# Plain float32 matmuls on unsplit weights in place of three float32r products of split halves, in a one-layer hybrid decoder kernel

## The chip, the cores and the metric

The kernel runs on one core of a Trainium2 chip. The metric is device time in microseconds (us) of one execution. Three runs of the kernel before took 1446.25, 1450.61 and 1451.01 us; their median is 1450.61 us.

## The reference, cut to what matters

One layer on 256 tokens of width 2048, batch 1, all float32: a mixer (half gated delta net, half RWKV7), a cross attention to 256 memory rows, and a squared-ReLU feed-forward part of width 8192.

```python
u = rmsnorm(h, mix_norm_w)
p = u @ w_in                                  # 2048 x 7440
h = h + concat(deltanet(p[:4112]), rwkv7(p[4112:])) @ w_out
h = h + cross_attention(rmsnorm(h), rmsnorm(mem), wq, wk, wv, wo)
u = rmsnorm(h, ffn_norm_w)
h = h + square(relu(u @ w1)) @ w2             # 2048 x 8192, 8192 x 2048
out = rmsnorm(h, final_norm_w)
```

Nearly all arithmetic is in the products with w_in, w_out, wq, wk, wv, wo, w1 and w2. They are the projections that the change is about. The mixer's scans, triangular inverses, transposes and attention scores are small float32 matmuls of their own, which the change leaves as they are.

## The kernel before, in words

Weights stream from HBM in blocks of 512 KB, each once: two k tiles of 128 rows by 512 columns, or for w1 eight k tiles by 128 columns. `weights` (L228) issues the DMA of a block into a tile `raw` (pool `wp`, five buffers) on SP's queue. It then splits the block in two parts, in two steps of 128x512: ScalarE casts the high half, `A.copy(hi, w)` (L239, tile `whi`), and VectorE subtracts it from the original to make the low half (L240, tile `wlo`, shown at L110, the line of the helper `tt`). Both halves have the type float32r. The activations are split in the same way, by `lhs_split` (L187, tile `xhl`), `tok_T` (L1035, tile `hhl`), `dn_out` (`dhl`), `split_out` (`ohl`), the attention's output (`oahi`, `oalo`) and `relu2` (L1186, tiles `fhi`, `flo`).

A projection is then three float32r products summed in PSUM: high by high, high by low, low by high. There are two forms.

- `gemm` (L244) puts tokens on the partitions of the result: for each k tile and each half of the tokens (m) three products of 128x128 by 128x512 (L254 to L256). It serves w_in, w_out, wq, wk, wv, wo and w2. `gemm_rows` (L205) is the same for the last 512 columns of w2, with the first 128 tokens done before the others.
- `gemm_T` (L261) puts columns of w1 on the partitions: for each k tile one product 512 columns wide, W_hi by (x_hi, x_lo) side by side (L273), and one 256 columns wide, W_lo by x_hi (L272, L275). The two halves of the 512-wide result are added after the sum, in `relu2`.

The low-rank group at the start (the loop at L393, "lora") has products 272 columns wide (L402 to L404).

Three PSUM banks (`ps_g`) serve these products. The order of all instructions on each engine comes from the Tile framework's scheduler, which fits the projections between the steps of the scans and inverses; `tc.high_priority(3000)` brings the loads and splits of weights forward. The first half of the program is the mixer, with w_in's products as filler between its small matmuls (`ps_s`, `ps_x`); then come output projection and cross attention, and from about 727 us on there is only the feed-forward part: four times 32 `gemm_T` groups of w1 and four `gemm` groups of w2.

The steps of the triangular inverse that the text names are, on TensorE, L541, L553, L558, L563 and L567: each works on what ScalarE and VectorE made of the step before. They have the lines L504, L516, L521, L526 and L530 after the change.

Of the kernel before, what the change touches and what calls it, by code (L numbers as in the profile page):

```python
# [10 lines left out]
F32R = mybir.dt.float32r  # L11
# [16 lines left out]
WB = 3  # L28
# [12 lines left out]
def host_layout(inp):  # L41
# [63 lines left out]
def body(ctx, tc, I, out, dbg=None, upto=99):  # L105
# [24 lines left out]
    wp = ctx.enter_context(tc.tile_pool(name="wp", bufs=5))  # L130
    lx = ctx.enter_context(tc.tile_pool(name="lx", bufs=4))
# [39 lines left out]
    # derived per-channel scalars  # L171
# [15 lines left out]
    def lhs_split(raws, wname, pool, tag):  # L187
        """raw^T (times the norm's weight) split in two float32r parts, four k tiles a tile, as they are asked for."""
        res = {}

        def get(kt, m):
            j = kt // 4
            if j not in res:
                raw = raws(j)
                t = pool.tile([P, 4, 2, S], F32R, tag=tag, bufs=4, name=nm("xhl"))
                for q in range(4):
                    w = C(wname, 4 * j + q)
                    act(t[:, q, 0], raw[:, q], AF.Copy, scale=w)
                    stt(t[:, q, 1], raw[:, q], w, t[:, q, 0].bitcast(F32), ALU.mult, ALU.subtract)
                res[j] = t  # L200
            return tuple(res[j][:, kt % 4, i, m * P:(m + 1) * P] for i in range(2))

        return get

    def gemm_rows(lhs, wblk, evac, kbs, his, los):  # L205
        """the same, the first 128 tokens before the others, from weights that all stay."""
        kbs, w = list(kbs), []
        for m in range(2):
            acc = bank("g")
            for i, kb in enumerate(kbs):  # L210
                if m == 0:
                    with tc.high_priority(3000):
                        raw = wp.tile([P, KB, NB], F32, tag="raw", name=nm("raw"))
                        nc.sync.dma_start(out=raw, in_=wblk[kb])
                        hi, lo = his(), los()
                        A.copy(hi, raw)
                        tt(lo, raw, hi.bitcast(F32), ALU.subtract)
                    w.append((hi, lo))
                hi, lo = w[i]
                for q in range(KB):  # L220
                    first, last = i == 0 and q == 0, i == len(kbs) - 1 and q == KB - 1
                    xh, xo = lhs(kb * KB + q, m)
                    T.matmul(acc, lhsT=xh, rhs=hi[:, q], start=first, stop=False)
                    T.matmul(acc, lhsT=xh, rhs=lo[:, q], start=False, stop=False)
                    T.matmul(acc, lhsT=xo, rhs=hi[:, q], start=False, stop=last)  # L225
            evac(m, acc)

    def weights(src, a, b, parts):  # L228
        """a block of weights [128, a, b] in two float32r parts."""
        with tc.high_priority(3000):  # L230
            raw = wp.tile([P, a, b], F32, tag="raw", name=nm("raw"))
            nc.sync.dma_start(out=raw, in_=src)
            res = []
            n = a // parts
# [9 lines left out]
    def gemm(lhs, wblk, n, evac, kbs=None):  # L244
        """[256 tok, n] = lhs^T @ W: three float32r products stand for the float32 one."""
        acc = [bank("g") for _ in range(2)]
        kbs = list(kbs if kbs is not None else range(NKT // KB))
        for kb in kbs:
            w = weights(wblk[kb], KB, n, KB)
            for q in range(KB):  # L250
                for m in range(2):
                    first, last = kb == kbs[0] and q == 0, kb == kbs[-1] and q == KB - 1
# [4 lines left out]
                    if last:  # L257
                        evac(m, acc[m][:, :n])


    def gemm_T(rhs, wblk, evac):  # L261
        """(x W)^T in four parts of 128 columns, [128 col, (W x_hi, W_hi x_lo)]; rhs(kt) is (x_hi, x_lo)^T, 512 wide."""
        for j in range(4):
            acc = bank("g")
            for b in range(2):
                w = weights(wblk[j, b], 8, P, 2)
                for k in range(8):
                    first, last = b == 0 and k == 0, b == 1 and k == 7
                    x = rhs(8 * b + k)
                    xf = x.rearrange("p a t -> p (a t)")  # L270
# [5 lines left out]
            evac(j, acc)  # L276
# [22 lines left out]
    def rms(src, name):  # L299
        """1 / rms of the rows of src[:, m, :]."""  # L300
# [8 lines left out]
    def tpose4(o, ins):  # L309
        """up to four 128x128 transposes into one bank."""  # L310
# [40 lines left out]
    xl = lhs_split(lambda j: xraw[:, 4 * j:4 * j + 4], "mixw", lx, "lx")  # L351
# [9 lines left out]
    # the clock of the array rises and the functions' table loads while the first operands are on their way  # L361
# [29 lines left out]
    with tc.manual_schedule(engines={mybir.EngineType.Activation, mybir.EngineType.DVE}):  # L391
        for kb in range(NKT // KB):
            raw = wl[kb]  # L393
            whi = sp_.tile([P, KB, LORA], F32R, tag="whi", bufs=3, name=nm("whi"))
            wlo = sp_.tile([P, KB, LORA], F32R, tag="wlo", bufs=3, name=nm("wlo"))
            A.copy(whi, raw)
            tt(wlo, raw, whi.bitcast(F32), ALU.subtract)
            for m in range(2):
                for q in range(KB):
                    first, last = kb == 0 and q == 0, kb == NKT // KB - 1 and q == KB - 1  # L400
                    xh, xo = xl(kb * KB + q, m)
                    T.matmul(acc[m], lhsT=xh, rhs=whi[:, q], start=first, stop=False)  # L402
                    T.matmul(acc[m], lhsT=xh, rhs=wlo[:, q], start=False, stop=False)
                    T.matmul(acc[m], lhsT=xo, rhs=whi[:, q], start=False, stop=last)  # L404
# [30 lines left out]
    # gates of the deltanet: [tok, chunk, head]  # L435
# [35 lines left out]
    inv = [0]  # L471

    def inverse(B, pool, pool2):
        """B is overwritten with the inverse of I + (its strictly upper part); what lies below its diagonal is zero.

        X12 = -X11 B12 X22 for blocks of 2 to 128, the larger ones on tiles of the array."""
# [11 lines left out]
        def quarters(t, n):  # L488
            """the quarters 11, 12, 22 of the diagonal blocks of 2n: [q, block, row, column]."""
# [94 lines left out]
    def rw_shift(pt, c0, names, blks):  # L584
        """columns c0.. of the projection [tok, col] to shifted [col, tok] tiles of two blocks."""
# [12 lines left out]
    def rw_unit(u, r, k, v):  # L598
# [59 lines left out]
        # bonus * v  # L658
# [8 lines left out]
        # scores  # L667
# [21 lines left out]
        # [tok, .] forms  # L689
# [57 lines left out]
        # group norm, bonus, gate  # L747
# [94 lines left out]
    def dn_unit(g, kq, v2):  # L842
# [6 lines left out]
        # norms per token: [tok, (k/q), chunk, head]  # L849
# [21 lines left out]
        # decays, scores  # L871
# [72 lines left out]
        # norm over the head, times silu(z)  # L944
# [16 lines left out]
    def dn_out(g, ob):  # L961
# [4 lines left out]
        t = lx.tile([P, 4, 2, S], F32R, tag="lx", name=nm("dhl"))  # L966
        for q in range(2):
            bb = bank()
            tpose4(bb, [ob[:, 4 * c + 2 * q + i] for i in range(2) for c in range(2)])
            b2 = bb.rearrange("p (a b) -> p a b", a=2)  # L970
            hi, lo = (t[:, 2 * q:2 * q + 2, i] for i in range(2))
            act(hi, b2, AF.Copy, scale=dnwh)
# [252 lines left out]
```

## Time and profile before

| | before |
|---|---|
| runs | 1446.25, 1450.61, 1451.01 us |
| median | 1450.61 us |
| profiled execution: span from its first to its last instruction | 1442.5 us |
| TensorE busy | 1414.8 us, 98% |
| VectorE busy | 950.1 us, 66% |
| ScalarE busy | 780.8 us, 54% |
| DMA | 252.88 MB, mean 175 GB/s |

The page gives the span of the profiled execution, and no time of its own for it beside that. The median of the runs is 8.1 us above the span, which is what lies around the span (start and end of the program). TensorE's matmuls are pipelined: the duration of one record (some 390 ns for 512 columns) is longer than the distance between the starts of two. So what one matmul costs is read from starts, not from durations.

### The profile page before, as it was taken

The numbers are of one execution on the slowest core, as the hardware profiler recorded it, in microseconds if no ns is written. First come the engines' busy times: TensorE is split into PE (matmuls) and PEld (weight loads), VectorE is DVE, ScalarE is ACT, GpSimd is POOL, SyncE is SP. The second block draws the span as 40 slices with busy tenths as digits, with TensorE's granted clock in tenths as the row PEclk, the third lists the DMA queues.
The fourth block names the chain that finished last, engine by engine and source line by source line (L and its number), as shares of the span: only waits on it lengthen the run. The fifth ranks groups of instructions, "written<-read, shape, count | busy, mean of one in ns | idle before, by whom it ended". The sixth has DMA issues, their size and how long they took to land.

```text
span 1442.5 us, 22496 instructions
## 1 busy us (share of the span) xinstructions
PE 1414.8 (98%) x8284; PEld 1168.9 (81%) x8284; DVE 950.1 (66%) x1799; ACT 780.8 (54%) x1491; POOL 50.6 (4%) x66
## 2 busy tenths in 40 slices
PE   9999999999999989999999999999999999999997
PEld 7877788787876868887788888888888888888886
DVE  7748574869587685767676655666556665566664
ACT  7656454555456454566565544555445554455553
POOL 0010001100010000000000000000000000000000
PEclk9999999999999999999999999999999999999999
DMA  7444433454366464556465556555665555655554
GB/s 281 157 145 152 135 121 112 147 177 144 102 200 207 138 190 146 166 173 212 136 209 186 190 192 197 185 187 189 193 197 186 185 190 194 195 182 187 191 188 146
DMA packets 90688, 252.88 MB, mean 175 GB/s; under 512 B 20673, under 2 KB 29393, under 8 KB 90193
## 3 DMA queue, kind: packets, MB, share of 16 engines
q1 hardware_dynamic: 70304, 243.96, 51.2%
q10 hardware_dynamic: 19920, 6.42, 1.8%
q8 instruction: 65, 1.06, 0.3%
q0 software_dynamic: 352, 1.06, 0.2%
q14 instruction: 47, 0.38, 0.1%
HBM read 244.72 MB, written 6.69 MB: 174 GB/s over the span
## 4 chain that ended last, share of the span: by engine, by line
PE 82%; DMA 7%; DVE 6%; ACT 3%; issue 2%; SPq 0%; POOL 0%; ACTq 0%; POOLq 0%; DVEq 0%
PE ps_g L273 16%; PE ps_g L255 16%; PE ps_g L254 15%; PE ps_g L256 15%; PE ps_g L272 8%; DVE wlo L110 2%; PE ps_s L675 2%; DMA scr<-Sc 1%; DMA xc<-inv 1%; DMA mraw<-in_memT_dram 1%; PE ps_x L312 1%; DMA g<-scr 1%; DVE xtmp L110 1%; DMA junk<-in_mem_dram 1%; PE ps_s L312 1%
## 5 line engine op out<-in xcount | busy, mean ns | idle before, releaser
L110 DVE TENSOR_TENSOR wlo<-raw,whi 128x512 fp32r<-128x512 f32 x848 | 583.3, 691 | 388.1 <-ACT whi L239 386.8
L239 ACT CAST whi<-raw 128x512 fp32r<-128x512 f32 x848 | 523.4, 621 | 489.8 <-DVE wlo L110 203.7
L273 PE MATMUL ps_g<-hhl,whi 128*128 128x512 f32 x1024 | 357.6, 398 | 0.2 <-ACT whi L239 0.2
L272 PE MATMUL ps_g<-hhl,wlo 128*128 128x256 f32 x960 | 269.9, 281 | 0.0
L273 PEld LDWEIGHTS ps_g<-hhl,whi 128*128 128x128 f32 x1024 | 188.4, 188 | 42.5 <-ACT whi L239 0.5
L255 PE MATMUL ps_g<-wlo,xhl 128*128 128x512 f32 x512 | 209.9, 410 | 8.4 <-DVE wlo L110 8.3
L256 PE MATMUL ps_g<-whi,xhl 128*128 128x512 f32 x512 | 202.0, 395 | 0.0
L256 PE MATMUL ps_g<-whi,flo 128*128 128x512 f32 x480 | 186.7, 389 | 0.0
L255 PE MATMUL ps_g<-wlo,fhi 128*128 128x512 f32 x480 | 186.7, 389 | 0.0
L254 PE MATMUL ps_g<-whi,xhl 128*128 128x512 f32 x512 | 180.8, 406 | 3.4 <-ACT whi L239 3.4
L272 PEld LDWEIGHTS ps_g<-hhl,wlo 128*128 128x128 f32 x960 | 181.5, 189 | 2.8 <-ACT hhl L122 0.2
L254 PE MATMUL ps_g<-whi,fhi 128*128 128x512 f32 x480 | 151.3, 389 | 0.0
L255 PEld LDWEIGHTS ps_g<-wlo,xhl 128*128 128x128 f32 x512 | 96.6, 189 | 37.7 <-DVE wlo L110 18.2
L254 PEld LDWEIGHTS ps_g<-whi,xhl 128*128 128x128 f32 x512 | 94.6, 189 | 26.7 <-ACT whi L239 5.9
L256 PEld LDWEIGHTS ps_g<-whi,xhl 128*128 128x128 f32 x512 | 96.7, 189 | 18.8 <-issue 0.7
L255 PEld LDWEIGHTS ps_g<-wlo,fhi 128*128 128x128 f32 x480 | 90.1, 188 | 18.8
L256 PEld LDWEIGHTS ps_g<-whi,flo 128*128 128x128 f32 x480 | 90.1, 188 | 18.7
L254 PEld LDWEIGHTS ps_g<-whi,fhi 128*128 128x128 f32 x480 | 90.1, 188 | 18.6
L113 DVE SCALAR_TENSOR_TENSOR cy<-ps_x,colt,cy 128x255 f32<-128x255 f32 (+2 forms) x72 | 34.2, 476 | 10.9 <-ACT cy L122 10.3
L1191 ACT CAST fhi<-hid 128x256 fp32r<-128x256 f32 x64 | 26.1, 408 | 9.5 <-DVE hid L113 0.8
L113 DVE SCALAR_TENSOR_TENSOR hid<-hid 128x256 f32<-128x256 f32 x64 | 27.2, 425 | 2.2
L113 DVE SCALAR_TENSOR_TENSOR h<-ps_g,rf,h 128x512 f32<-128x512 f32 (+1 forms) x34 | 22.8, 712 | 8.0 <-PE ps_g L225 8.0
(360 smaller groups left out, 1540.7 us busy)
## 6 DMA issues: line engine op xcount, KB each, us to landing
raw<-in_w_dram SPq DMA_DIRECT2D x256, 512.0 KB, 3.5
raw<-in_w_in_dram SPq DMA_DIRECT2D x112, 512.0 KB, 3.5
raw<-in_w_out_dram SPq DMA_DIRECT2D x32, 512.0 KB, 3.5
raw<-in_wk_dram SPq DMA_DIRECT2D x8, 512.0 KB, 3.5
mraw<-in_memT_dram SPq DMA_DIRECT2D x8, 512.0 KB, 3.6
raw<-in_wq_dram SPq DMA_DIRECT2D x8, 512.0 KB, 3.4
raw<-in_wv_dram SPq DMA_DIRECT2D x8, 512.0 KB, 3.7
raw<-in_wo_dram SPq DMA_DIRECT2D x8, 512.0 KB, 3.5
```

The source lines that it names most:

```text
L110: return (e or V).tensor_tensor(o, a, b, op=op)
L113: return V.scalar_tensor_tensor(o, a, s, b, op0=op0, op1=op1)
L239: A.copy(hi, w)
L254: T.matmul(acc[m][:, :n], lhsT=xh, rhs=w[q][0], start=first, stop=False)
L255: T.matmul(acc[m][:, :n], lhsT=xh, rhs=w[q][1], start=False, stop=False)
L256: T.matmul(acc[m][:, :n], lhsT=xl, rhs=w[q][0], start=False, stop=last)
L272: T.matmul(acc[:, 0:S], lhsT=w[k][1], rhs=x[:, 0], start=False, stop=False)
L273: T.matmul(acc, lhsT=w[k][0], rhs=xf, start=first, stop=last)
L312: T.transpose(out=o[:, j * P:(j + 1) * P], in_=a, identity=ident)
L675: T.matmul(bb[hl][:, 256 * i:256 * i + 256], lhsT=BK[hs, j, i, cs], rhs=AR[hs, j, :, cs], start=True, stop=True)
L1191: A.copy(hi[:, j], t)
```

## The change

All splitting goes. `weights` is the DMA alone, and its tile `raw`, plain float32, is the operand. `gemm` and `gemm_rows` issue one plain float32 matmul per k tile and token half in place of three float32r ones; `gemm_T` issues one of 256 columns in place of a 512 and a 256 column one; the lora loop one in place of three. Activations are scaled by the norm's weight only, with the scaling shared between ScalarE and VectorE. `relu2` reads the 256 finished columns, one ReLU on ScalarE and one square on VectorE, in place of five instructions. `split_out` loads its tile by DMA without a split. The pools `wp` and `lx` have eight buffers each (5 and 4 before; the tiles of `lx` are half as large).

```diff
-    wp = ctx.enter_context(tc.tile_pool(name="wp", bufs=5))
-    lx = ctx.enter_context(tc.tile_pool(name="lx", bufs=4))
+    wp = ctx.enter_context(tc.tile_pool(name="wp", bufs=8))
+    lx = ctx.enter_context(tc.tile_pool(name="lx", bufs=8))
...
-    def weights(src, a, b, parts):
+    def weights(src, a, b, pool=None, tag="raw", **kw):
         with tc.high_priority(3000):
-            raw = wp.tile([P, a, b], F32, tag="raw", name=nm("raw"))
+            raw = (pool or wp).tile([P, a, b], F32, tag=tag, name=nm("raw"), **kw)
             nc.sync.dma_start(out=raw, in_=src)
-            for q in range(parts):
-                hi = wp.tile([P, n, b], F32R, tag="whi", bufs=WB, name=nm("whi"))
-                lo = wp.tile([P, n, b], F32R, tag="wlo", bufs=WB, name=nm("wlo"))
-                w = raw[:, q * n:(q + 1) * n]
-                A.copy(hi, w)
-                tt(lo, w, hi.bitcast(F32), ALU.subtract)
-                res += [(hi[:, i], lo[:, i]) for i in range(n)]
-        return res
+        return raw
...
     def gemm(lhs, wblk, n, evac, kbs=None):
-                    xh, xl = lhs(kb * KB + q, m)
-                    T.matmul(acc[m][:, :n], lhsT=xh, rhs=w[q][0], start=first, stop=False)
-                    T.matmul(acc[m][:, :n], lhsT=xh, rhs=w[q][1], start=False, stop=False)
-                    T.matmul(acc[m][:, :n], lhsT=xl, rhs=w[q][0], start=False, stop=last)
+                    T.matmul(acc[m][:, :n], lhsT=lhs(kb * KB + q, m), rhs=w[:, q], start=first, stop=last)
...
     def gemm_T(rhs, wblk, evac):
-                    if not first:
-                        T.matmul(acc[:, 0:S], lhsT=w[k][1], rhs=x[:, 0], start=False, stop=False)
-                    T.matmul(acc, lhsT=w[k][0], rhs=xf, start=first, stop=last)
-                    if first:
-                        T.matmul(acc[:, 0:S], lhsT=w[k][1], rhs=x[:, 0], start=False, stop=False)
+                    T.matmul(acc[:, 0:S], lhsT=w[:, k], rhs=rhs(8 * b + k), start=b == 0 and k == 0,
+                             stop=b == 1 and k == 7)
...
             def relu2(j, p):
                 t = ptp.tile([P, S], F32, tag="pt", name=nm("hid"))
-                A.copy(t, p[:, S:])
-                tt(t, p[:, 0:S], t, ALU.add)
-                stt(t, t, 0.0, t, ALU.max, ALU.mult)
-                A.copy(hi[:, j], t)
-                tt(lo[:, j], t, hi[:, j].bitcast(F32), ALU.subtract)
+                act(t, p, AF.Relu)
+                tt(hid[:, j], t, t, ALU.mult)
```

The scheduler writes a new order with it. Two places on TensorE matter for the prediction.

The first is a stretch of w1 in the feed-forward part. Before, each k tile is a pair of rows, the 512-column product with the high half of the weights and the 256-column product with the low half:

```order
L272 MATMUL ps_g_12779<-hhl_7406,wlo_12809 128x256
L273 MATMUL ps_g_12779<-hhl_7406,whi_12808 128x512
L272 MATMUL ps_g_12779<-hhl_7473,wlo_12813 128x256
L273 MATMUL ps_g_12779<-hhl_7473,whi_12812 128x512
L272 MATMUL ps_g_12779<-hhl_7473,wlo_12813 128x256
```

After the change four k tiles are one row of four alike, from the loaded weights themselves (`raw`), and a group of 16 k tiles is four rows:

```order
L245 MATMUL ps_g_4562<-hhl_4374,raw_4563 128x256 x4
L245 MATMUL ps_g_4562<-hhl_4405,raw_4563 128x256 x4
L245 MATMUL ps_g_4562<-hhl_4436,raw_4573 128x256 x4
L245 MATMUL ps_g_4562<-hhl_4467,raw_4573 128x256 x4
L245 MATMUL ps_g_4586<-hhl_4374,raw_4587 128x256 x4
```

No other work stands between the groups in either order.

The second is the third of the six triangular inverses, in the mixer (`Sc_95` is its matrix, `ps_g` rows are w_in's products, L675 and L638 the scores of the next unit). Before, the step L563 is followed by this, up to L567:

```order
L563 MATMUL ps_s_469_2474<-Y_2472,Sc_95 64x64 x8
L675 MATMUL ps_s_564_2882<-AR_2811,BK_2810 128x256 x2
L312 MATMUL ps_s_565_2893<-cons,BK_2810 128x128 x4
L254 MATMUL ps_g_3612<-whi_3642,xhl_153 128x512
L255 MATMUL ps_g_3612<-wlo_3643,xhl_153 128x512
L256 MATMUL ps_g_3612<-whi_3642,xhl_153 128x512
L254 MATMUL ps_g_3613<-whi_3642,xhl_153 128x512
L255 MATMUL ps_g_3613<-wlo_3643,xhl_153 128x512
L256 MATMUL ps_g_3613<-whi_3642,xhl_153 128x512
```

Eight more products of w_in follow these nine rows before L567. After the change, all of the steps from L516 to L530 stand within nine rows, with no product of w_in between them:

```order
L504 MATMUL ps_s_288_1668<-b_287_1666,Sc_95 32x32 x16
L638 MATMUL ps_s_352_1978<-AR_1931,BK_1930 128x256 x2
L638 MATMUL ps_s_353_1989<-AR_1931,BK_1930 128x256 x2
L221 MATMUL ps_g_2920<-raw_2964,xs_188 128x512 x2
L516 MATMUL ps_s_290_1692<-b_283_1593,b_289_1685 32x32 x16
L638 MATMUL ps_s_354_1990<-AR_1931,BK_1930 128x256 x2
L638 MATMUL ps_s_355_2001<-AR_1931,BK_1930 128x256 x2
L521 MATMUL ps_s_291_1711<-cons,Sc_95 64x64 x8
L638 MATMUL ps_s_356_2002<-AR_1931,BK_1930 128x256 x2
L283 MATMUL ps_s_357_2013<-cons,BK_1930 128x128 x4
L526 MATMUL ps_s_293_1722<-Y_1720,Sc_95 64x64 x8
L283 MATMUL ps_s_359_2020<-cons,sh_v_1433 128x128 x4
```

The row after these is the step L530. The other five inverses keep products of w_in between most of their steps.

## Rows read from the trace of the kernel before

**Rows 1.** The page's busy time and the shares of the chain that ended last, by engine.

```profile
PE 1414.8 (98%) x8284; PEld 1168.9 (81%) x8284; DVE 950.1 (66%) x1799; ACT 780.8 (54%) x1491; POOL 50.6 (4%) x66
...
PE 82%; DMA 7%; DVE 6%; ACT 3%; issue 2%; SPq 0%; POOL 0%; ACTq 0%; POOLq 0%; DVEq 0%
```

**Rows 2.** Windows: us, busy us (instructions) of each engine, granted clock, DMA share, GB/s.

```profile
0.00:727.00 727.00, 707.67 (x4719) 569.72 (x4720) 506.71 (x1048) 412.83 (x833) 48.77 (x63) 1.00 0.50 163
727.00:1424.00 697.00, 696.79 (x3523) 590.97 (x3522) 439.26 (x741) 363.53 (x649) 0.70 (x1) 1.00 0.58 190
1424.00:1442.50 18.50, 10.35 (x46) 8.20 (x44) 4.14 (x11) 4.47 (x12) 1.11 (x2) 0.87 0.32 114
```

**Rows 3.** Waits of TensorE, whole span: us in total, times, longest us.

```profile
PE ps_g L255 <- DVE wlo L110: 8.3, 12, 2.5
PE ps_g L254 <- ACT whi L239: 3.4, 4, 1.6
```

**Rows 4.** Timeline of TensorE in w1: start us, us, what, count.

```profile
799.81 0.40 PE L273 MATMUL ps_g<-hhl,whi 128*128 128x512 f32 x1
800.05 0.28 PE L272 MATMUL ps_g<-hhl,wlo 128*128 128x256 f32 x1
...
803.35 0.62 PE L273 MATMUL ps_g<-hhl,whi 128*128 128x512 f32 x2
```

**Rows 5.** The same in w2.

```profile
999.98 0.39 PE L255 MATMUL ps_g<-wlo,fhi 128*128 128x512 f32 x1
...
1003.60 0.39 PE L255 MATMUL ps_g<-wlo,fhi 128*128 128x512 f32 x1
```

**Rows 6.** DMA issues by tensor (in_w is w1 and w2): count, KB each, us to landing.

```profile
raw<-in_w_dram SPq DMA_DIRECT2D x256, 512.0 KB, 3.5
raw<-in_w_in_dram SPq DMA_DIRECT2D x112, 512.0 KB, 3.5
raw<-in_w_out_dram SPq DMA_DIRECT2D x32, 512.0 KB, 3.5
raw<-in_wk_dram SPq DMA_DIRECT2D x8, 512.0 KB, 3.5
```

**Rows 7.** Instructions of line 1081, plain float32, 256 columns: ns min/median/max, first and last start.

```profile
L1081 PE MATMUL ps_s<-KT,qT x12: 377/378/379, 669.1 to 676.0; 128*128 128x256 f32 x12
L1081 PE MATMUL ps_x<-KT,qT x4: 379/379/379, 670.0 to 670.6; 128*128 128x256 f32 x4
```

**Rows 8.** Timeline of TensorE there.

```profile
669.12 1.02 PE L1081 MATMUL ps_s<-KT,qT 128*128 128x256 f32 x4
669.99 1.03 PE L1081 MATMUL ps_x<-KT,qT 128*128 128x256 f32 x4
```

**Rows 9.** Chain that ended last, in order of time: start us, us, what, count.

```profile
366.71 1.73 PE ps_s L857 x16
...
416.43 1.73 PE ps_s L887 x8
...
539.35 0.62 PE ps_s L541 x32
...
556.27 1.07 PE ps_s L567 x16
```

**Rows 10.** Groups by line and form: busy us, mean ns of one | idle before, releaser.

```profile
L857 PE MATMUL ps_s<-cons,sq 128*128 128x1 f32 x64 | 8.0, 250 | 1.0 <-ACT sq L122 1.0
L887 PE MATMUL ps_s<-kq 128*128 128x256 f32 x32 | 9.3, 421 | 0.0
L110 DVE TENSOR_TENSOR wlo<-raw,whi 128x512 fp32r<-128x512 f32 x848 | 583.3, 691 | 388.1 <-ACT whi L239 386.8
L239 ACT CAST whi<-raw 128x512 fp32r<-128x512 f32 x848 | 523.4, 621 | 489.8 <-DVE wlo L110 203.7
L273 PEld LDWEIGHTS ps_g<-hhl,whi 128*128 128x128 f32 x1024 | 188.4, 188 | 42.5 <-ACT whi L239 0.5
```

**Rows 11.** Windows of TensorE alone: us, busy us (instructions), granted clock, DMA share, GB/s.

```profile
360.00:420.00 60.00, 59.64 (x342) 0.97 0.41 133
```

More of the change, by code (lines that the diff above doesn't have):

```diff
@@ L194, in get, with gemm, gemm_rows @@
                 raw = raws(j)
-                t = pool.tile([P, 4, 2, S], F32R, tag=tag, bufs=4, name=nm("xhl"))
+                t = pool.tile([P, 4, S], F32, tag=tag, name=nm("xs"))
                 for q in range(4):
                     w = C(wname, 4 * j + q)
-                    act(t[:, q, 0], raw[:, q], AF.Copy, scale=w)
-                    stt(t[:, q, 1], raw[:, q], w, t[:, q, 0].bitcast(F32), ALU.mult, ALU.subtract)
+                    if q % 2:
+                        ts(t[:, q], raw[:, q], w, ALU.mult)
+                    else:
+                        act(t[:, q], raw[:, q], AF.Copy, scale=w)
                 res[j] = t
-            return tuple(res[j][:, kt % 4, i, m * P:(m + 1) * P] for i in range(2))
+            return res[j][:, kt % 4, m * P:(m + 1) * P]
         return get
-    def gemm_rows(lhs, wblk, evac, kbs, his, los):
+    def weights(src, a, b, pool=None, tag="raw", **kw):
+        with tc.high_priority(3000):
+            raw = (pool or wp).tile([P, a, b], F32, tag=tag, name=nm("raw"), **kw)
+            nc.sync.dma_start(out=raw, in_=src)
+        return raw
+    def gemm(lhs, wblk, n, evac, kbs=None):
+        acc = [bank("g") for _ in range(2)]
+        kbs = list(kbs if kbs is not None else range(NKT // KB))
+        for kb in kbs:
+            w = weights(wblk[kb], KB, n)
+            for q in range(KB):
+                for m in range(2):
+                    first, last = kb == kbs[0] and q == 0, kb == kbs[-1] and q == KB - 1
+                    T.matmul(acc[m][:, :n], lhsT=lhs(kb * KB + q, m), rhs=w[:, q], start=first, stop=last)
+                    if last:
+                        evac(m, acc[m][:, :n])
+    def gemm_rows(lhs, wblk, evac, kbs, pool):
         kbs, w = list(kbs), []
@@ L211, in gemm_rows @@
                 if m == 0:
[L212 to L219, printed above, removed]
+                    w.append(weights(wblk[kb], KB, NB, pool, f"lw{i}"))
@@ L220, in gemm_rows @@
                 for q in range(KB):
                     first, last = i == 0 and q == 0, i == len(kbs) - 1 and q == KB - 1
[L222 to L225, printed above, removed]
+                    T.matmul(acc, lhsT=lhs(kb * KB + q, m), rhs=w[i][:, q], start=first, stop=last)
@@ L400, in body @@
                     first, last = kb == 0 and q == 0, kb == NKT // KB - 1 and q == KB - 1
[L401 to L404, printed above, removed]
+                    T.matmul(acc[m], lhsT=xl(kb * KB + q, m), rhs=wl[kb][:, q], start=first, stop=last)
         for j in range(4):
@@ L965, in dn_out @@
         stream[0] = g
-        t = lx.tile([P, 4, 2, S], F32R, tag="lx", name=nm("dhl"))
+        t = lx.tile([P, 4, S], F32, tag="lx", name=nm("dhl"))
         for q in range(2):
@@ L978, in split_out @@
     def split_out(j):
-        raw = wp.tile([P, 4, S], F32, tag="raw", name=nm("oraw"))
-        nc.sync.dma_start(out=raw, in_=o_dram[4 * j:4 * j + 4].rearrange("b p t -> p b t"))
-        t = lx.tile([P, 4, 2, S], F32R, tag="lx", name=nm("ohl"))
-        A.copy(t[:, :, 0], raw)
-        tt(t[:, :, 1], raw, t[:, :, 0].bitcast(F32), ALU.subtract)
+        t = lx.tile([P, 4, S], F32, tag="lx", name=nm("ohl"))
+        nc.sync.dma_start(out=t, in_=o_dram[4 * j:4 * j + 4].rearrange("b p t -> p b t"))
         sp[2 + j] = t
@@ L1026, in lo_T @@
     def lo_T(kt, m):
-        return tuple(sp[kt // 4][:, kt % 4, i, m * P:(m + 1) * P] for i in range(2))
+        return sp[kt // 4][:, kt % 4, m * P:(m + 1) * P]
     def add_h(gcol):
@@ L1071, in body @@
     pt = pts()
-    gemm(lambda kt, m: tuple(hl(kt)[:, i, m * P:(m + 1) * P] for i in range(2)), I["wq"][0], NB, evac_tok(rq, pt))
+    gemm(lambda kt, m: hl(kt)[:, m * P:(m + 1) * P], I["wq"][0], NB, evac_tok(rq, pt))
     stream[0] = None
@@ L1100, in body @@
             T.matmul(bb[:, 0:S], lhsT=Vm[:, t, i * P:(i + 1) * P], rhs=pT[:, t], start=t == 0, stop=t == 1)
[L1101 to L1105 removed]
+        oa[i] = xa.tile([P, S], F32, name=nm("oa"))
+        A.copy(oa[i], bb[:, 0:S])
     make, hl = tok_T(h, "ffnw")
     for gcol in range(4):
[L1108 removed]
+        gemm(lambda kt, m: oa[kt][:, m * P:(m + 1) * P], I["wo"][gcol], NB, add_h(gcol),
              kbs=range(2))
@@ L1199, in body @@
             if ch == 3 and gcol == 3:
-                gemm_rows(hid_T, I["w2"][gcol], last, kbs,
-                          lambda: next(lhi),
-                          lambda: next(llo))
+                gemm_rows(hid_T, I["w2"][gcol], last, kbs, fp)
             else:
```

76 lines of the change are left out of this document (13 added, 63 removed).

## The prediction, written before the changed kernel was run

> **What bounds the kernel now.** I read the page first. TensorE (PE) is busy for 98% of the span and carries 82% of the chain that ended last; VectorE (DVE) has 66% and ScalarE (ACT) 54% [rows 1]. A busy PE alone proves little, since its records overlap, so the windows come next. In the feed-forward part PE has no gap at all, 696.79 of 697 us, and the granted clock is 1.00, the 2.4 GHz level; in the mixer and attention before it PE is busy for 707.67 of 727 us [rows 2]. The waits agree: what PE waits for the two halves of the weights is 8.3 and 3.4 us in the whole span [rows 3]. So the time is the sum of what PE's matmuls occupy, and the starts say how much that is.
>
> In w1, ten pairs lie between the starts at 799.81 and 803.35 us: 0.354 us a pair of 512 and 256 columns [rows 4]. In w2, sixteen products lie between 999.98 and 1003.60: 0.226 us each, 0.679 us for three [rows 5]. 512 columns at 2.4 GHz are 0.213 us, so a float32r product costs one pass and some 13 ns. A check: the feed-forward part has 512 threes and 1024 pairs, 348 + 363 = 710 us, and the trace has 697 us of it and some 10 more behind 1424 us [rows 2].
>
> **What a plain float32 matmul costs.** The kernel has small ones already. Line 1081 issues eight matmuls of 256 columns (four heads, two token halves), and the trace has 12 + 4 = 16 records for them [rows 7]: two records a matmul. Four such records start at 669.12 and the next four at 669.99, 0.87 us for two matmuls [rows 8]; eight records of line 887, also of 256 columns [rows 10], take 1.73 us, 0.216 each [rows 9]. 256 columns at 2.4 GHz are 0.107 us, so each record streams its columns twice. A plain matmul makes four passes, with only some 2 ns beside them. The loads of the array do not show in this: the sixteen records of line 857 are one column wide [rows 10] and come 0.108 us apart [rows 9], which bounds what a load takes; half of 0.216, it hides under a 256-column record.
>
> So three passes (768 columns a k tile in w1, 1536 in w2) become four. Per k tile:
> - w2's form: no plain record of 512 columns is in the trace. Two passes of 512 are 0.427 us; with the 2 ns seen at 256 columns 0.429, with the 13 ns of the float32r product 0.440. I take 0.429, from the nearest plain rows: 0.858 us a matmul (bounds 0.853 to 0.880).
> - w1's form: two records of 256 columns, 0.431 us (bounds 0.427 to 0.453).
>
> **The sum, part by part.**
> - All products of `gemm` and `gemm_rows`: 112 + 32 + four times 8 blocks, and half of the 256 blocks named in_w [rows 6], are 304, four k tile and token half pairs each: 1216 x (0.858 - 0.679) = +218 us.
> - `gemm_T`: 128 blocks of eight k tiles, 1024 x (0.431 - 0.354) = +79 us.
> - The lora loop: 96 passes of 272 columns with 12 ns each, 12.0 us, become 64 records of twice 272 columns, 14.6 us (an estimate by columns from the same rows): +3 us.
> - The splits go: 848 of DVE, 583.3 us, and 848 of ACT, 523.4 us [rows 10], and three of five instructions of `relu2`. All this lay under PE's work, and what it cost is PE's waits for it, 8.3 + 3.4 us [rows 3]: -12 us. The rest brings nothing. What covers it is PE itself, so if PE were faster the splits would count; it gets slower.
> - The weights. SP issues the same blocks; a `raw` buffer is now free only when the matmuls have read it. A block feeds PE for 4 x 0.858 = 3.4 us where it fed 2.7, so the need falls from 190 GB/s [rows 2] to some 153, and eight buffers reach 27 us ahead against 3.5 us to landing [rows 6]. I cost it at nothing; PE's longer work hides it.
> - `split_out` loses its two splits and has a DMA straight into the operand, the same bytes from the same queue. Nothing: what is saved behind the DMA is part of the idle time before 727 us [rows 2], which I leave out of the sum but for the 12 us above.
> - The order. In the third inverse the steps L504 to L530 now stand close together. What PE has between them is ten score matmuls (at most 0.43 us each), two products of w_in (1.7), eight transposes (0.9) and the steps, about 8 us. The quickest passage over the same steps before is 539.35 to 556.27, 17 us, with other work in between [rows 9]. So PE may wait there for ACT and DVE between nothing and 9 us; both are far less loaded than before, and I take the middle, +5 us.
>
> Sum: 218 + 79 + 3 - 12 + 5 = +293 us (rounded terms; unrounded 292). On the profiled span of 1442.5 us that is 1735; the median of the runs is 8.1 us above the span, so **1743 us**.
>
> Here a page would have it otherwise. The Trainium skill, TensorE: Matmul & The Clock Gate, section on the back-to-back issue gap, has 518 cycles, 216 ns, for 512 columns. If that held for every pass, the change would cost one more pass of 216 ns in w2's form, +263 us instead of 218, and the forecast would be near 1790 by that term alone. The float32r rows here say 226, ten more than the page, so part of what the fourth pass costs is given back by the overhead of products that go; the measurement decides, and I give that figure no chance beside rival 1, which ends at the same time for another reason.
>
> **The rivals.**
> 1. *The 13 ns stay.* If each record of a plain matmul pays the overhead of a float32r product, 2432 records of 512 columns pay 11 ns more than I take and 2048 of 256 columns 10.5: +27 +22, 1791 us. For it: the cause of the 13 ns is not in the trace. Against it: the plain records of 256 columns show 2. Chance 0.08.
> 2. *Waits in the mixer.* The scans and inverses are chains over PE, ACT, DVE and DMA, and PE's order is fixed by the scheduler. If what I price in the third inverse comes in each of the six at its upper end, that is 6 x 9 = 54 us, +49: 1792 us. It decides where PE's work between two steps is shorter than the other engines' part. Against it: the fill between the steps is now a third longer, and ACT and DVE lose most of their load. Chance 0.07.
> 3. *The loads of the array pace it, and the change is faster.* A load is 188 ns [rows 10], and the loads are busy for 81% [rows 1]. Three loads a k tile in w2's form become two, in w1's they stay two: 1216 fewer, 1216 x 0.188 = 229 us less, 1222 us. It would decide if two starts could not come closer than one load. Against it, strongly: starts lie 0.108 us apart at one column [rows 9], below 0.188, and in w1 the step from a 512-column to a 256-column product is 0.24 us [rows 4], which follows the columns. Chance 0.01. The Trainium skill, Perfetto Trace Analysis, section on identifying the most-contended engine, would judge TensorE's headroom by this very share of the loads; here the starts do not follow it.
> 4. *The plain matmul streams its columns fewer times than line 1081 suggests.* The change breaks even if a plain product of 512 columns takes 0.69 us (1728 products' worth of columns against 826 + 363 us now, less 4 for the waits and the rest); with two passes, 0.429, it would be 446 us faster, about 1000 us. Against it are all plain rows [rows 7 to 9], so it needs the projections to be built otherwise than line 1081, which uses the same call on the same type. Chance 0.02.
> 5. *The clock.* Plain float32 comes today in pieces of a few us; a window in which one-column matmuls stand [rows 9] shows 0.97 [rows 11]. If long plain streams were granted the 1.2 GHz level, PE's 1485 us in projections would double, past 3000 us. Against it: PE stays without gaps. Chance 0.01.
>
> **How the numbers follow.** The forecast, four passes and a PE that stays the bound, has 0.81; rivals 1 to 5 have 0.19. The lower end takes plain records at 0.427 and 0.213 us (-10), all of PE's 19 us of idle time before 727 us as recovered instead of 12 (-8), no wait in the third inverse (-5) and the lowest run instead of the median (-4): 1716, which I round to 1715. The upper end goes to rivals 1 and 2, taken singly: 1790. Within 0.3%, about what a measurement of this kernel can tell from no change, I put 0.01, faster 0.02, slower 0.97.
>
> **What would show it.** Right: two records per projection matmul; starts in w2 0.429 us apart and in w1 0.2155; PE at 98% or more with the clock at 1.00; DVE and ACT below 25%; DMA near 150 GB/s; the feed-forward part 707 + 92 + 79 = 878 us. Step by step, the split's waits are gone from PE's list, and a wait of some us shows at L516 to L530. Wrong: starts of 0.44 (rival 1), waits of PE for ACT or DVE of 30 us or more in the mixer (rival 2), a clock below 1.00 in the feed-forward part (rival 5), or one record per matmul or passes at half the columns (rivals 3 and 4).

## The result, and the profile after

The changed kernel takes 1744.03 us in the median of four runs (1738.8 to 1744.98), against 1450.81 us before: a ratio of 1.2018, with a 95% interval from 1.1989 to 1.2046. The forecast was 1743. The profiled execution took 1744.98 us, its span (first to last instruction) is 1743.3.

The page's busy time and the chain that ended last, of the changed kernel, answer to [rows 1]:

```profile
PE 1713.7 (98%) x7036; PEld 1035.8 (59%) x7036; DVE 322.9 (19%) x757; ACT 223.1 (13%) x521; POOL 48.5 (3%) x66
...
PE 94%; DMA 2%; DVE 1%; issue 1%; ACT 1%; POOL 0%; POOLq 0%; ACTq 0%; DVEq 0%; SPq 0%
PE ps_g L221 57%; PE ps_g L245 25%; PE ps_s L638 1%; PE ps_x L283 1%; DMA junk<-in_mem_dram 1%; PE ps_s L367 1%; PE ps_g L235 1%; PE ps_s L283 1%; DMA mraw<-in_memT_dram 1%; DMA scr<-Bm 1%; PE ps_s L820 0%; PE ps_s L695 0%; PE ps_s L850 0%; PE ps_s L526 0%; PE ps_s L694 0%
```

PE is as busy as before; what has changed is that hardly anything else is on the chain, and that VectorE and ScalarE have lost two thirds and more of their work. The load share (PEld) fell from 81% to 59% while the kernel became slower.

Groups of TensorE in the feed-forward part (line, tiles, shape and count | busy us, mean ns), changed kernel:

```profile
L245 PE MATMUL ps_g<-hhl,raw 128*128 128x256 f32 x2048 | 443.1, 379 | 0.0
L221 PE MATMUL ps_g<-raw,fhid 128*128 128x512 f32 x960 | 412.6, 592 | 0.0
```

w1 has 1024 k tile steps and 2048 records, w2's `gemm` 480 matmuls and 960 records: two records a matmul, as at line 1081 before [rows 7]. The timeline of TensorE merges them now, since nothing stands between (start us, us, what, count):

```profile
999.71 10.46 PE L221 MATMUL ps_g<-raw,fhid 128*128 128x512 f32 x24
...
1129.64 20.67 PE L245 MATMUL ps_g<-hhl,raw 128*128 128x256 f32 x95
```

From the start of the first to the start of the last: (10.46 - 0.59) / 23 = 0.429 us a record of 512 columns, and (20.67 - 0.38) / 94 = 0.216 of 256 (the mean durations of the groups above taken off for the last record). Before, one float32r product was 0.226 [rows 5] and a pair 0.354 [rows 4].

Windows of the changed kernel, cut where w1 begins and where the last product ends, answer to [rows 2]:

```profile
0.00:852.00 852.00, 830.89 (x3954) 451.31 (x3955) 261.21 (x634) 187.33 (x427) 46.72 (x63) 0.97 0.42 139
852.00:1735.00 883.00, 882.81 (x3084) 584.52 (x3082) 59.51 (x119) 33.48 (x88) 1.24 (x2) 1.00 0.45 151
```

The same cut of the kernel before lies at 722 and 1434 us:

```profile
0.00:722.00 722.00, 702.67 (x4689) 565.32 (x4690) 502.68 (x1041) 408.22 (x821) 48.77 (x63) 1.00 0.50 162
722.00:1434.00 712.00, 711.79 (x3597) 603.57 (x3595) 445.08 (x753) 370.37 (x665) 1.25 (x2) 1.00 0.57 189
```

So the feed-forward part costs 883 - 712 = 171 us more, what was forecast (92 + 79). The part ahead of it costs 852 - 722 = 130 us more, where the terms of the forecast give 704 x 0.179 + 3 - 12 + 5 = 122. And here the granted clock is 0.97 in place of 1.00. Of the 130, 2 are idle time of TensorE (852 - 830.89 = 21.1 us against 722 - 702.67 = 19.3) and 128 are busy time. The same windows over the projections' products alone (tile ps_g: us, busy us of TensorE, clock, DMA share, GB/s), before and after:

```profile
0.00:722.00 722.00, 532.59 (x2109) 1.00 0.50 162
```

```profile
0.00:852.00 852.00, 633.67 (x1408) 0.97 0.42 139
```

They became 101 us dearer ahead of w1, where 704 x 0.179 = 126 was priced, and all other work of TensorE there 27 us, where 3 was priced. (The busy time of a group holds the tail of a record that the next one overlaps, so this division is rough.)

The waits of TensorE (us in total, times, longest) answer to [rows 3]:

```profile
PE ps_s L283 <- DVE ob L108: 7.3, 1, 7.3
PE ps_s L492 <- DVE b L487: 5.0, 1, 5.0
PE ps_x L283 <- DVE cy L111: 2.2, 1, 2.2
```

The waits for split weights are gone, as forecast; three others have taken their place. The granted clock shows four stretches inside the program at 0.50. Windows over them (us, busy us of PE, PEld, DVE, ACT, POOL, clock, DMA share, GB/s):

```profile
378.50:385.30 6.80, 6.80 (x33) 6.73 (x33) 5.03 (x14) 2.79 (x6) 0.00 (x0) 0.50 0.11 11
443.30:457.00 13.70, 13.70 (x50) 8.76 (x48) 4.21 (x12) 2.63 (x5) 3.26 (x2) 0.50 0.11 40
576.40:590.10 13.70, 10.69 (x154) 8.51 (x155) 4.22 (x15) 2.51 (x6) 3.27 (x2) 0.50 0.06 7
699.30:709.60 10.30, 5.74 (x13) 3.06 (x14) 3.02 (x6) 1.33 (x2) 1.64 (x1) 0.50 0.00 0
```

All four are at the 1.2 GHz level, 44.5 us together, with PE busy for 36.9 of them. At full clock this work would take at least half of that, so they cost at most 18 us. The profile of before has two such stretches, at 373 and 465 us, some 7 us together.

What one of them costs can be read from a second execution of the same program (`after_again`, below), which kept the full clock from 430 to 460 us:

```profile
430.00:460.00 30.00, 30.00 (x193) 18.39 (x186) 10.41 (x24) 8.67 (x17) 3.27 (x2) 1.00 0.38 129
```

From the inverse's step L521 to the next products of L850 the first execution, then the second, has (start us, us, what, count):

```profile
443.09 0.88 PE L521 MATMUL ps_s<-cons,Sc 64*64 64x64 f32 x8
...
459.37 0.81 PE L850 MATMUL ps_s<-kq 128*128 128x256 f32 x3
```

```profile
443.17 0.63 PE L521 MATMUL ps_s<-cons,Sc 64*64 64x64 f32 x8
...
452.97 1.03 PE L850 MATMUL ps_s<-kq 128*128 128x256 f32 x4
```

The same work takes 16.3 and 9.8 us: 13.7 us at half the clock cost 6.5 us here, nearly half, because PE was busy all through. And whether a stretch at half the clock comes differs from one execution of a kernel to the next.

### The profile page after: what moved, and what is told of

Same layout as the page of the kernel before. It is cut to its first block, busy times and chain, and to the rows that moved or that the text cites. A ratio compares the mean times of both kernels' runs of the same rounds, so it can differ in the third digit from the quotient of the medians.

```text
span 1743.3 us, 16914 instructions
## 1 busy us (share of the span) xinstructions
PE 1713.7 (98%) x7036; PEld 1035.8 (59%) x7036; DVE 322.9 (19%) x757; ACT 223.1 (13%) x521; POOL 48.5 (3%) x66
## 4 chain that ended last, share of the span: by engine, by line
PE 94%; DMA 2%; DVE 1%; issue 1%; ACT 1%; POOL 0%; POOLq 0%; ACTq 0%; DVEq 0%; SPq 0%
PE ps_g L221 57%; PE ps_g L245 25%; PE ps_s L638 1%; PE ps_x L283 1%; DMA junk<-in_mem_dram 1%; PE ps_s L367 1%; PE ps_g L235 1%; PE ps_s L283 1%; DMA mraw<-in_memT_dram 1%; DMA scr<-Bm 1%; PE ps_s L820 0%; PE ps_s L695 0%; PE ps_s L850 0%; PE ps_s L526 0%; PE ps_s L694 0%
## 5 line engine op out<-in xcount | busy, mean ns | idle before, releaser
L221 PE MATMUL ps_g<-raw,xs 128*128 128x512 f32 x1024 | 461.5, 601 | 0.0
L245 PE MATMUL ps_g<-hhl,raw 128*128 128x256 f32 x2048 | 443.1, 379 | 0.0
L245 PEld LDWEIGHTS ps_g<-hhl,raw 128*128 128x128 f32 x2048 | 388.8, 190 | 54.0 <-issue 1.4
L221 PE MATMUL ps_g<-raw,fhid 128*128 128x512 f32 x960 | 412.6, 592 | 0.0
L221 PEld LDWEIGHTS ps_g<-raw,xs 128*128 128x128 f32 x1024 | 191.0, 192 | 213.9 <-issue 210.6
L221 PEld LDWEIGHTS ps_g<-raw,fhid 128*128 128x128 f32 x960 | 182.4, 190 | 227.9 <-issue 226.7
L221 PE MATMUL ps_g<-raw,dhl 128*128 128x512 f32 x128 | 57.9, 609 | 0.1
L221 PE MATMUL ps_g<-raw,ohl 128*128 128x512 f32 x128 | 57.5, 598 | 0.0
L221 PE MATMUL ps_g<-raw,oa 128*128 128x512 f32 x64 | 29.0, 596 | 0.5 <-ACT oa L1056 0.5
L221 PE MATMUL ps_g<-raw,hhl 128*128 128x512 f32 x64 | 28.8, 592 | 0.0
L235 PE MATMUL ps_g<-raw,fhid 128*128 128x512 f32 x64 | 27.6, 592 | 0.0
L638 PE MATMUL ps_s<-AR,BK 64*128 64x256 f32 x128 | 26.1, 402 | 0.4 <-ACT Sc L643 0.4
```

The lines of the kernel that those rows point to most:

```text
L221: T.matmul(acc[m][:, :n], lhsT=lhs(kb * KB + q, m), rhs=w[:, q], start=first, stop=last)
L235: T.matmul(acc, lhsT=lhs(kb * KB + q, m), rhs=w[i][:, q], start=first, stop=last)
L245: T.matmul(acc[:, 0:S], lhsT=w[:, k], rhs=rhs(8 * b + k), start=b == 0 and k == 0, stop=b == 1 and k == 7)
L638: T.matmul(bb[hl][:, 256 * i:256 * i + 256], lhsT=BK[hs, j, i, cs], rhs=AR[hs, j, :, cs], start=True, stop=True)
```

## The experiments

Two theories stood against each other: that the passes over the array set the time and the rest is a few us, or that a good part of the 293 us lies in the mixer's order, in waits and in what ACT and DVE do. The runs take the change apart by projection, put the splits back, and carry the count of passes to two and to one; the last four look at the lower clock. Each kernel was timed beside the kernel before.

**w1 alone.** In the kernel before, `gemm_T` and its operands as in the change:

```diff
-                w = weights(wblk[j, b], 8, P, 2)
+                    w = wp.tile([P, 8, P], F32, tag="raw", name=nm("raw"))
+                    nc.sync.dma_start(out=w, in_=wblk[j, b])
...
+                    T.matmul(acc[:, 0:S], lhsT=w[:, k], rhs=x, start=first, stop=last)
```

> The kernel before with the change made in w1 alone (plain 256-column matmuls on the loaded weights and unsplit activations); all other projections keep their three float32r products. Theory (four passes of 256 columns, 0.431 us, in place of the pair's 0.354): +79 us, 1530 us, between 1524 and 1536. Rival (the cost of the change sits in the mixer's order and its waits, not in the passes): within 20 us of before.

Measured: 1530.02 us (1527.54 to 1532.35), 1.0566 of before (1.0539 to 1.0593), 81 us more than the 1449.01 of the kernel before. Its windows:

```profile
0.00:722.00 722.00, 701.66 (x4682) 565.33 (x4683) 497.90 (x1030) 407.25 (x818) 49.04 (x63) 0.99 0.48 162
722.00:1517.00 795.00, 794.63 (x3604) 679.72 (x3602) 255.79 (x428) 218.77 (x412) 1.25 (x2) 1.00 0.49 170
```

The whole difference is in the feed-forward part, 795 - 712 = 83 us, with 79 expected; the part before it takes the same 722 us. The theory's price for w1 holds.

**All but w1.** The changed kernel with w1's split and its pair of float32r products put back (five `raw` buffers, four larger `lx` tiles as before):

```diff
-                    T.matmul(acc[:, 0:S], lhsT=w[:, k], rhs=rhs(8 * b + k), start=b == 0 and k == 0,
-                             stop=b == 1 and k == 7)
+                    T.matmul(acc[:, 0:S], lhsT=w[k][1], rhs=x[:, 0], start=False, stop=False)
+                    T.matmul(acc, lhsT=w[k][0], rhs=xf, start=first, stop=last)
```

> The other half of w1_plain: every projection but w1 as in the changed kernel, w1 with its float32r pair on split weights and activations as before. Theory (each form costs its own passes): 1216 x (0.858 - 0.679) = 218 us and 3 for the lora loop on top of before, 1670 us, between 1662 and 1680, so that this kernel and w1_plain together make up the changed one's difference within 10 us. Rival (the forms interact: what the mixer loses in clock and waits comes only when all splits are gone): 15 us or more away from 1670.

Measured: 1652.95 us (1651.39 to 1655.7), 1.1422 of before (1.1391 to 1.1453), 205 us more than the 1448.3 beside it. That is 17 us below the expected value, outside the range that I gave. Its windows:

```profile
0.00:841.00 841.00, 824.89 (x3955) 447.37 (x3956) 264.67 (x641) 190.20 (x432) 46.76 (x63) 0.98 0.43 139
841.00:1643.00 802.00, 801.92 (x3083) 509.07 (x3081) 252.68 (x439) 184.98 (x349) 1.24 (x2) 1.00 0.50 168
```

The feed-forward part takes 802 - 712 = 90 us more, with 512 x 0.179 = 92 expected. Together with w1's 83 that is 173, beside the changed kernel's 171: in this part the projections' prices add up. Most of the miss is in the first part: it takes 841 - 722 = 119 us more, where 126 + 3 were expected (the expectation, unlike the forecast, took nothing off for the waits of [rows 3]). Some 4 us more lie between profile and median: the spans of the two profiled executions differ by 1651.6 - 1442.5 = 209 us, the medians by 205. The changed kernel, with the same matmuls in the first part, has 852 there. The pools differ, so the scheduler's order differs, and so do the waits. This order has no wait of 5.0 us at the inverse's first step. Its list begins with

```profile
PE ps_s L299 <- DVE ob L109: 6.9, 2, 6.5
PE ps_s L711 <- DVE ze L109: 1.4, 1, 1.4
```

and the rest of it are 1.2 us and less. Of the 11 us, 5 are idle time of PE (21.1 us against 841 - 824.89 = 16.1) and 6 busy time. How much of this is order and buffers is not shown, since one stretch at half the clock moved 6.5 us between two executions of the changed kernel itself.

**The splits put back.** In the changed kernel, in `weights`:

```diff
+                A.copy(hf[:, c], flat[:, c])
+                tt(lf[:, c], flat[:, c], hf[:, c], ALU.subtract)
-        return raw
+        return hi
```

> The changed kernel with the two steps of the split put back on every block of weights of gemm and gemm_T, in plain float32: ScalarE copies the block, VectorE subtracts the copy from it, and the matmuls read the copy; the result of the subtraction is not read. Four raw buffers and three copies in place of eight raw buffers. Theory (ACT and DVE work lies under PE): between 0 and +12 us on the changed kernel's 1744, so 1744 to 1756. Rival (a good part of what the change cost or gave came from ACT and DVE being in the way of the mixer's chains): +20 us or more.

Measured: 1746.65 us (1741.99 to 1748.01), 1.2050 of before (1.2020 to 1.2080), beside 1.2018 of the changed kernel. The groups of the two steps (line, what, count | busy us, mean ns | idle before, releaser):

```profile
L109 DVE TENSOR_TENSOR wlo<-raw,whi 128x512 f32<-128x512 f32 x848 | 550.1, 687 | 659.8 <-ACT whi L220 658.4 <-issue 0.3
L220 ACT COPY whi<-raw 128x512 f32<-128x512 f32 x848 | 481.6, 616 | 759.6 <-PE ps_g L233 418.9 <-PE ps_g L257 276.8 <-issue 37.3
```

More than 1000 us of work on two engines make 3 us, inside the measurement. Under the products of the changed kernel the splits are covered by PE, and their absence is worth nothing by itself. Under shorter products it is otherwise, as the next run shows.

**Two products in place of three.** In the kernel before:

```diff
                     T.matmul(acc[m][:, :n], lhsT=xh, rhs=w[q][0], start=first, stop=False)
-                    T.matmul(acc[m][:, :n], lhsT=xh, rhs=w[q][1], start=False, stop=False)
-                    T.matmul(acc[m][:, :n], lhsT=xl, rhs=w[q][0], start=False, stop=last)
+                    T.matmul(acc[m][:, :n], lhsT=xh, rhs=w[q][1], start=False, stop=last)
```

> The kernel before without the product of the low half of the activations with the high half of the weights, in every projection but the lora group (that part of the result is left out; the low halves of the activations are still made). Theory (passes over the array set the time): two float32r products of 0.226 us a k tile and token half in w2's form, two of 256 columns of 0.118 us a k tile in w1, so 1216 x 0.226 + 1024 x (0.354 - 0.236) = 396 us less than before: 1055 us, up to 1100 where the weights' DMA, which would have to bring 512 KB in 1.8 us, holds it up. Rival (the loads of the array pace it): 1216 loads fewer, 229 us less, 1222 us.

Measured: 1141.85 us (1134.42 to 1143.15), 0.7871 of before (0.7841 to 0.7900). This is 42 us above the range. The rival's 1222 is excluded: with 1216 loads fewer than before the kernel gains 307 us, where the loads alone would have given 229. The feed-forward part alone has 512 x 2 + 1024 x 2 = 3072 loads, which at 0.188 us each would take 577 us; it takes 484. The windows, cut at w1's beginning, say where the theory missed:

```profile
0.00:643.00 643.00, 585.22 (x3982) 457.89 (x3983) 492.10 (x1038) 401.79 (x819) 54.21 (x63) 0.93 0.55 182
643.00:1127.00 484.00, 482.30 (x3078) 436.53 (x3077) 411.71 (x686) 356.93 (x661) 0.70 (x1) 1.00 0.82 276
```

The feed-forward part has 484 us, where 512 x 0.452 + 1024 x 0.236 is 473: near the passes. The first part has 643, where 722 - 704 x 0.226 is 563: the shorter w_in products no longer cover the chains of the scans. PE is idle for 643 - 585 = 58 us there, against 19 before, the clock is 0.93, and the two largest groups of its waits are for the splits (us in total, times, longest):

```profile
PE ps_g L254 <- DVE wlo L110: 18.1, 15, 3.2
PE ps_g L253 <- ACT whi L238: 13.0, 9, 4.4
```

**One product.** As above, with the second product gone too, the low halves of the weights not made, six buffers for the high halves in place of three, and

```diff
-                A.copy(hi, w)
-                tt(lo, w, hi.bitcast(F32), ALU.subtract)
+                if q % 2:
+                    V.tensor_copy(hi, w)
+                else:
+                    A.copy(hi, w)
```

> The kernel before with only the product of the two high halves in every projection but the lora group, the low halves of the weights not made and the casts of the weights shared between ScalarE and VectorE (what the low halves add is left out of the result). Theory (passes): PE needs 1216 x 0.226 + 1024 x 0.118 = 396 us for the projections and some 250 for the rest, about 650; then the DMA is next: 252.9 MB at the 281 GB/s of the first slice of the profile of before are 900 us, so 880 to 960 us with PE waiting for raw weights. Rival (PE stays the bound, since the DMA can go faster than it has been asked to): 650 to 750 us.

Measured: 926.64 us (923.3 to 932.09), 0.6399 of before (0.6373 to 0.6426). It is inside the range, and of all kernels here it is the fastest, faster than before and the changed kernel, for a result that leaves the low halves out. But the reason is not the one I gave, and that the time fits is luck:

```profile
0.00:572.00 572.00, 466.82 (x3277) 365.00 (x3278) 344.26 (x860) 298.08 (x641) 47.59 (x63) 0.81 0.60 204
572.00:910.00 338.00, 295.57 (x1545) 215.00 (x1542) 179.73 (x432) 208.63 (x414) 0.69 (x1) 0.99 1.01 395
```

In the feed-forward part the DMA engines are the bound, at a share of 1.01, but they move 395 GB/s and not 281. The first part is not bound by DMA (0.60): PE is idle for 572 - 467 = 105 us there, in waits for DVE and ACT of up to 9.5 us, and the clock is 0.81.

**Wide sums.** In the changed kernel, at the 1-column matmuls near two of the low-clock stretches:

```diff
-                    T.matmul(bs[:, o:o + 1], lhsT=sq[:, j, c * P:(c + 1) * P], rhs=ones[:, 0:1],
+                    T.matmul(bs[:, 32 * o:32 * o + 32], lhsT=sq[:, j, c * P:(c + 1) * P], rhs=ones[:, 0:32],
```

> The changed kernel with the 64 one-column records of line 820 (sums over a head's channels, the matrix times a column of ones) made 32 columns wide; only the first column of each 32 is read. A record of a plain matmul is 0.11 us apart from the next at 1 and at 128 columns alike, so the matmuls themselves take the same time. The profile of the changed kernel has four stretches at half the granted clock inside the program, two of them (at 443 and 576 us) around these records. Theory (the clock falls because the array is little used by one-column matmuls): these two stretches go, and the time falls by 5 to 14 us. Rival (it falls because PE waits in these places, for DVE 5.0 us at L492): the stretch at 576 stays, and the time changes by less than 4 us.

Measured: 1741.35 us (1738.96 to 1745.57), 1.2039 of before (1.2008 to 1.2070): the same as the changed kernel within the interval. Windows around the two stretches, first the changed kernel:

```profile
430.00:460.00 30.00, 30.00 (x149) 18.11 (x144) 9.39 (x22) 7.81 (x15) 3.26 (x2) 0.77 0.32 103
566.00:592.00 26.00, 19.05 (x190) 13.33 (x190) 13.58 (x40) 3.74 (x8) 3.27 (x2) 0.74 0.36 125
```

and with the wide sums:

```profile
430.00:460.00 30.00, 30.00 (x201) 18.39 (x195) 10.28 (x24) 8.67 (x17) 3.27 (x2) 1.00 0.37 130
566.00:592.00 26.00, 20.44 (x223) 14.72 (x224) 8.49 (x25) 3.87 (x9) 3.28 (x2) 0.74 0.18 56
```

The first stretch is gone. But it is gone in the second profile of the unedited kernel too (clock 1.00 from 430 to 460 us, shown with the result), so this does not speak for the wide sums. The second, with its 5 us wait at L492, stays, and the time changes by less than 4 us, as the rival has it. That one-column matmuls lower the clock is not shown.

**More buffers for w_in's results.** In the changed kernel:

```diff
-    wp = ctx.enter_context(tc.tile_pool(name="wp", bufs=8))
+    wp = ctx.enter_context(tc.tile_pool(name="wp", bufs=7))
-    ptp = ctx.enter_context(tc.tile_pool(name="ptp", bufs=4))
+    ptp = ctx.enter_context(tc.tile_pool(name="ptp", bufs=6))
```

> The changed kernel with six buffers in the pool that the results of w_in go to (ptp) in place of four, and seven weight buffers in place of eight. The order then has products of w_in between the steps L504 to L530 of the third inverse, which stood without them. Theory (the steps left bare cost both PE's waits and, right behind, a stretch at half the clock, 378 to 385 us): that stretch goes, and 4 to 12 us with it, 1732 to 1740 us. Rival (the order is a zero-sum of fillers: what is put here is missing later): within 4 us of 1744, with low-clock stretches elsewhere.

Measured: 1740.16 us (1739.54 to 1741.18), 1.2030 of before (1.2003 to 1.2057). Windows over the third inverse, first the changed kernel, then this one:

```profile
370.00:390.00 20.00, 19.09 (x116) 15.00 (x115) 13.38 (x35) 8.79 (x20) 1.91 (x3) 0.83 0.21 58
```

```profile
370.00:390.00 20.00, 20.00 (x107) 9.80 (x106) 4.01 (x8) 5.04 (x12) 1.92 (x3) 1.00 0.61 214
```

With products of w_in between its steps, this stretch keeps the full clock. All three profiles in which the steps stand bare as in the changed kernel (its two and that of the wide sums) have a stretch at half the clock here, and both with six buffers have none. But the time is not told apart from the changed kernel's, and low-clock stretches come elsewhere, as the rival has it: from 600 to 640 us the clock is 0.91 and from 660 to 690 us 0.94, where the changed kernel has 1.00.

**Both edits, beside the changed kernel.** Five rounds each.

> The changed kernel with both edits, six buffers for the results of w_in and the 32-column sums of line 820. Theory (the half-clock stretches are paid for by what PE did before them, and these two edits fill two of the places): fewer such stretches than the changed kernel has, 4 to 12 us below after_again. Rival (fillers are moved, not gained): within 3 us of after_again.

> The changed kernel once more, to stand beside ptp6_wide on one chip. 1739 to 1745 us.

Measured: 1738.71 us (1737.3 to 1746.68), 1.2021 of before (1.1991 to 1.2051), against 1744.18 us (1741.93 to 1745.02), 1.2051 (1.2023 to 1.2079). The medians lie 5.5 us apart, the intervals overlap, and one run of the edited kernel is above all of the other's. So this stays unclear; by the medians it is 0.3%. There are not fewer stretches at half the clock: the profile of the kernel with both edits has four inside the program, some 30 us together, and that of `after_again` three, some 37 us.

## Why the prediction was right

- **Passes.** Two records a matmul, 0.429 us for 512 columns and 0.216 for 256, against 0.429 and 0.2155 taken. Of the bounds that I had for the 512-column record, 0.427 to 0.440, the nearest plain rows were the right guide, and the float32r product's 13 ns the wrong one (rival 1). The feed-forward part's +171 us is the sum of the two terms, and PE stayed the bound. This part of the hit is no luck.
- **The first part.** Its sum came out at 130 us for 122, but not term by term. The products took 101 us more where 126 was priced, PE's other work 27 where 3 was priced. Up to 15 us of the two together can be the lower clock (at most 18 after, 3 before). Why the products became less dear than their distances in w2 say, and the other work dearer, no run here shows. That the two nearly cancel is luck.
- **The waits.** The terms for PE's waits, -12 for the splits and +5 for the order, made -7; measured is +2 of idle time. This is the term that was mis-sized, by 9 us. The splits' waits did go, but 7.3, 5.0 and 2.2 us of others came, at places where PE has to have what DVE makes in the mixer. The +5 us were priced in the third inverse: there the passage from L504 to L530 took 9.6 us with 0.4 us of waits, and what followed was 6.8 us at half the clock.
- **The splits.** "The rest brings nothing" holds: put back, they cost 3 us.
- **The clock.** I gave a lower clock in the plain streams 0.01, and rightly: they keep 1.00. But the four stretches of half clock in the mixer, 44.5 us together, were in no term; they cost at most 18 us, before has two, and one stretch of 13.7 us cost 6.5.
- **From the span to the median.** The 8.1 us between the span and the median of before are not what lies around the span. In every later run the time is 1.7 to 2.2 us above the span of the same execution (here 1744.98 - 1743.3 = 1.7). The other 6.4 us say that the profiled execution of before was a quick one. Of 25 later executions of before, on three chips, the three with a mean granted clock of 0.997 took 1443.98 to 1444.37 us and the three at 0.990 and below 1452.29 to 1453.24. So the change cost 1743.3 - 1442.5 = 301 us from profile to profile and 1744.03 - 1450.81 = 293 us from median to median, with 292 forecast. The sum is 9 us short by the one measure and right to 1 us by the other, since the profile of before is a quick execution and that of the changed kernel is not. That the median fits to 1 us is luck at this scale; the 171 us of the feed-forward part are not.
- **Rivals.** That the loads pace the array is excluded by the two-product kernel, and by the changed kernel itself, whose loads fell from 8284 to 7036 while it became slower. The Trainium skill, Perfetto Trace Analysis, section on identifying the most-contended engine, judges TensorE's headroom by MFU (the achieved share of its peak arithmetic) and by the loads' share. Here the loads' share went from 81% to 59% while PE stayed the bound and the time rose by 20%, so by itself that share does not tell what sets this kernel's time. Waits of 9 us in each of six inverses (rival 2) did not come; the longest single waits are 7.3 and 5.0 us. Two slips in the numbers: rivals 1 and 2 come out at 1791 and 1792, just above the range they were to set, and rivals 3 and 4, both faster, add up to 0.03 where "faster" has 0.02.

## What to carry to other kernels

Where PE has no gaps, count passes times columns from the distance between starts: three float32r products beat one plain float32 matmul, since the latter makes four passes, and the work of splitting costs little as long as ACT and DVE stay under PE (12 us of waits before, 3 us put back after). Look in the trace for the same kind of instruction elsewhere in the kernel before you price a new one; eight small plain matmuls gave the price of the feed-forward part's products to some us. What fewer passes save is had nearly in full only in the stage that has nothing but products (484 us beside 473 with two products, until with one the DMA engines bind): in the mixer the passes were also the cover of the scans' chains, and with two products in place of three, waits and a lower clock took back 80 us of what they gave. Before a profile is used as the base of a forecast, compare its time with the median; here 6.4 of the 8.1 us between them belonged to that one execution.

## What the runs showed of the hardware that was not expected

- A float32r product costs one pass and some 13 ns in w2's form of 512 columns (0.226 us) and at 256 columns (0.120), a record of a plain matmul 2 ns. In w1's pair the 512-column product takes 0.354 - 0.120 = 0.234 us, 21 ns above its columns. In the two-product kernel 256-column products follow each other at 0.12 us (0.107 by columns):

```profile
899.73 0.28 PE L268 MATMUL ps_g<-hhl,whi 128*128 128x256 f32 x1
899.85 0.28 PE L269 MATMUL ps_g<-hhl,wlo 128*128 128x256 f32 x1
899.97 0.28 PE L268 MATMUL ps_g<-hhl,whi 128*128 128x256 f32 x1
```

  Why, no run here tells.
- The clock falls to 1.2 GHz in the mixer without long gaps on PE: from 443 to 457 us PE is busy all the time. The same program kept 2.4 GHz there in its second profile, with the same work ahead of that place: products of w_in up to 439 us, then the step L516 and sixteen one-column records. The mean clock of the part ahead of w1 is 1.00 before, 0.97 after the change, 0.93 with two products and 0.81 with one. What it follows is open.
- The DMA engines moved 395 GB/s on one core over 338 us with blocks of 512 KB, where the kernel before moved 281 at most in a slice of its page. A slice is 36 us long; from 10 to 20 us the trace of before has 410 GB/s at a share of 1.03, so a shorter window would have shown this rate before the run. The Trainium skill, Perfetto Trace Analysis, section Roofline, puts the ceiling of one core's 16 engines at about 435 GB/s; at a share of 1.01 this trace comes to nine tenths of it.
